# A two-layer hybrid backbone in float32r: work tiles at multiples of 2 KB in their partition

## The chip, the cores and the metric

One core of one Trainium2 chip. The time is device microseconds of one execution, the median of several runs. A core has TensorE (matmuls; PE in the views, its weight loads PEld), VectorE (DVE), ScalarE (ACT), GpSimd (POOL) and SyncE (SP, which issues loads here). Operands lie in SBUF, 128 partitions of which each holds a row of bytes. A tile has the same start address in every partition, and that address is what this case is about.

## The reference

A backbone for a generator over 256 latent tokens with 256 context tokens, width 1024, two layers. All weights and activations are float32. Of the code what is computed:

```python
for i in range(DEPTH):
    x = ffn_half_step(x, ...)            # s + 0.5 * m * (silu(h @ w1) * (h @ w3)) @ w2, d_ff 2816
    ctx = ffn_half_step(ctx, ...)
    h_c = modulate(rmsnorm(ctx, ...), ...)
    h = modulate(rmsnorm(x, ...), ...)
    p_l = split_columns(h @ w_in[i], IN_SIZES)     # and the same for h_c
    o_l, _, _ = gla_mixer(...)           # bidirectional chunked gated linear attention
    y = merge(h, (o_l, spatial_gating(...), fourier_mix(...), short_conv(...)), ...)
    x = x + m_lat[5] * y                 # merge: sum of sigmoid(h @ w_gate[k]) * (branch[k] @ w_branch[k]), @ w_out
    x = ffn_half_step(x, ...)
    # and the context stream likewise, but for the second layer's last steps
return rmsnorm(x, g_final)
```

## The kernel before

Activations stand with channels on partitions and tokens along the row: `x` is 128 x 8 x 512 (eight groups of 128 channels; the 256 latent and the 256 context tokens side by side). The second layer's later stages work on the latent half alone, so matmuls there have 256 columns instead of 512.

A float32 product is made of three float32r matmuls (line 317, in `passes`): each operand is split into a high part, rounded to float32r, and a low part, the rest; high by high, high by low and low by high are summed in PSUM. The streamed operand (`rhs`) is an activation: `hh`/`hl` is the normalised input of a stage, split; `gh`/`gl` the gated hidden units of a feed-forward block (and, from the same buffers, the branch outputs `b0h` to `b3l` and `mh`/`ml`); `mhi`/`mlo` the second half of the merged branches. The stationary operand (`lhsT`) is a 128 x 128 slice, 512 bytes of a row, of a weight tile. Only `natural` (line 863) has them the other way around: weights are streamed, `hh`/`hl` are stationary. Some small products stay in plain float32 (lines 643, 705, 744, 777, 778, 942, 984 to 995).

A weight tile is 128 x 1024 (4 KB of a row). SyncE loads it into one of four `raw` buffers, ScalarE rounds it into one of four `whi` (line 78), VectorE or GpSimd writes the rest into one of four `wlo` (line 81). The class `_Program` holds the order: units are listed in the order of the computation, each takes its weight tiles, and `ahead` and `release` issue loads and splits as ring places come free. Modulation vectors (`ada_unit`, line 286) are woven in between by a table of rates, and the attention scan (`gla_stream`) runs as a generator that is ticked by TensorE's issued columns.

SBUF tiles come from two pools, `const` and `work`. A pool lays its tiles one after the other in the order of their first use, `work` behind `const`. All tiles of one name and buffer number have one place. In the built program the starts are, in bytes within a partition:

| tiles (in this order) | start before | past a multiple of 2 KB | start after | past a multiple of 2 KB |
|---|---|---|---|---|
| `x` | 21952 | 1472 | 22528 | 0 |
| X, Y, F, Q, K, A of the scan; `ada_raw`, `mlo` in the same places | 38336 to 58816 | 1472 | 38912 to 59392 | 0 |
| `sq`/`aT`, `sq7`/`a2`, the five `tmp` buffers | 62912 to 75200 | 1472 | 63488 to 75776 | 0 |
| `hh`, `hl` | 77248, 93632 | 1472 | 77824, 94208 | 0 |
| two `ms` of 64 bytes | 110016, 110080 | 1472, 1536 | 21056, 21120 (in `const`) | 576, 640 |
| `raw`, `whi`, `wlo`, four of each | 110144 to 155200 | 1600 | 110592 to 155648 | 0 |
| `v`/`mhi`, the `gh`/`gl` buffers | 159296 to 196160 | 1600 | 159744 to 196608 | 0 |
| `Sa`, `wsgu`, `bsgu`, `z`/`m0` | 200256 to 208448 | 1600 | 200704 to 208896 | 0 |
| `bst`, `bag`, `lnr` | 216640 to 217152 | 1600, 1984, 64 | 217088 to 217600 | 0, 384, 512 |
| `four`/`m1`, `Sf` | 217216, 225408 | 128 | 217664, 225856 | 576 |

1472 and 1600 are both 64 past a multiple of 128. Slices within these tiles are at multiples of 512 or 1024 bytes from the start, in the largest weight tile of `natural` at multiples of 1152.

Of the kernel before, what the change touches and what calls it, by code (L numbers as in the profile page):

```python
# [7 lines left out]
F32 = mybir.dt.float32  # L8
# [10 lines left out]
CTX = (256, 256)  # L19
BOTH = (0, 512)  # L20
EPS = 1e-6
HOLD = 4
DPOOL = 1
HPOOL = ((), (0, 1, 2, 3), (0, 1))
# [151 lines left out]
def kernel(ctx: ExitStack, tc: tile.TileContext, I, out: bass.AP):  # L176
# [3 lines left out]
    cp = ctx.enter_context(tc.tile_pool(name="const", bufs=1))  # L180
    pool = ctx.enter_context(tc.tile_pool(name="work", bufs=1))
# [4 lines left out]
    def mm_ps(name="mm"):  # L186
        return ps.tile([128, 512], F32, tag="mm", name=name, bufs=5)

    def sm_ps(name="sm"):
        return ps.tile([128, 512], F32, tag="sm", name=name, bufs=3)  # L190
# [4 lines left out]
    def const(name, shape, eng=S):  # L195
        t = cp.tile(shape, F32, tag=name, name=name)
        eng.dma_start(out=t, in_=I[name])
        return t


    x = pool.tile([128, KT, 512], F32, tag="x", name="x")
    cvec = const("cvec", [128, KT, 2])
    ident = const("ident", [128, 128])
    gnorm = const("gnorm", [128, 6, KT])
    bada = const("bada", [128, 2, 72])
    ones = cp.tile([128, 128], F32, tag="ones", name="ones")
# [170 lines left out]
    class Norm:  # L377
# [6 lines left out]
        def ms(self, c):  # L384
            c0 = c[0]
            p = self.p[c] = sm_ps("ms")
            for u in range(2):
                for i, sq in enumerate((st8["sq"], st8["sq7"])):
                    T.matmul(p[:, u:u + 1], lhsT=sq[:, c0 + 128 * u:c0 + 128 * u + 128],
                             rhs=ones[:, 0:1], start=(i == 0), stop=(i == 1))  # L390
            ms = self.r = pool.tile([128, 16], F32, tag="ms", name="ms", bufs=2)
            V.tensor_scalar(ms[:, 0:2], p[:, 0:2], 1.0 / D, EPS, ALU.mult, ALU.add)
            G.tensor_tensor(ms[:, 2:4], ms[:, 0:2], mhalf[:, 0:2], ALU.pow)

# [136 lines left out]
    def add_ffn(l, s, m, streams, after, weave, nxt):  # L531
# [36 lines left out]
        def down(ds_, f0, nf, last):  # L568

            def fn(*ws):  # L570
                ps_ = [sm_ps("dn") if l == 0 and f0 == 0 and d > HOLD else mm_ps() for d in ds_]
                cuts = [(0, nf - 2), (nf - 2, 2)] if len(ds_) > 1 else [(0, nf)]
                for k0, n in cuts:
                    for w2, p in zip(ws, ps_):
                        passes(p, rng, w2, lambda k: gs[f0 + k0 + k], k0, n, k0 == 0, k0 + n == nf)
                        if k0 + n == nf:
                            P.release()
                for d, p in zip(ds_, ps_):
                    if l == 0 and f0 == 0 and d < HOLD:
                        gs["held"] = gs.get("held", []) + [(p, d)]  # L580
                        continue
                    for ph, dh in gs.pop("held", []):
                        residual(ph, dh, rng, gate)
                    residual(p, d, rng, gate)
                    if last:
                        add_sq(d, rng)
                        after(d, rng)
# [42 lines left out]
    def gla_stream(l, c, A, want_o):  # L630
# [142 lines left out]
        for u, Su in ((0, S0), (1, S1)):  # L773
            p = sm_ps("o")
            for h in range(4):
                hs = slice(128 * h, 128 * h + 128)
                T.matmul(p[:, hs], lhsT=M[:, u, h, :], rhs=v[:, 2 * st + u, hs], start=True, stop=False)
                T.matmul(p[:, hs], lhsT=Q[:, h, 128 * u:128 * u + 128], rhs=Su[:, h, :], start=False, stop=True)
            sq = Yf[:, 512 * u:512 * u + 512]
            S.activation(out=sq, in_=p, func=AF.Square)  # L780
            ms = pool.tile([128, 16], F32, tag="ms", name="oms", bufs=2)
            V.tensor_reduce(ms[:, 0:4], sq.rearrange("p (h e) -> p h e", h=4), mybir.AxisListType.X, ALU.add)
            V.tensor_scalar(ms[:, 4:8], ms[:, 0:4], 1.0 / 128, EPS, ALU.mult, ALU.add)
            G.tensor_tensor(ms[:, 8:12], ms[:, 4:8], mhalf[:, 0:4], ALU.pow)
            V.tensor_tensor(Wr[:, :, c0 + 128 * u:c0 + 128 * u + 128], p.rearrange("p (h e) -> p h e", h=4),
                            ms[:, 8:12].unsqueeze(2).to_broadcast([128, 4, 128]), ALU.mult)
            yield

    def gla_all(l, A, want_ctx):
        yield from gla_stream(l, CTX, A, want_ctx)  # L790
        yield
        yield from gla_stream(l, LAT, A, True)


    def add_mixer(l, both, after, weave, nxt):
# [120 lines left out]
        def spread():  # L916
            n = 4 * ntt
            A["rs"] = pool.tile([128, 16], F32, tag="lnr", name="lnr")
            V.tensor_scalar(A["rs"][:, 0:n], A["bag"][:, 0:n, 1], EPS, None, ALU.add)
            G.tensor_tensor(A["rs"][:, 0:n], A["rs"][:, 0:n], mhalf[:, 0:n], ALU.pow)  # L920
# [445 lines left out]
```

## Time and profile before

| | us |
|---|---|
| median of 3 runs | 2304.64 (2300.55 to 2306.05) |
| the profiled execution | 2305.67 |
| its span, first to last instruction | 2303.7 |
| TensorE busy | 2239.5 |
| VectorE, ScalarE, GpSimd busy | 1364.8, 770.8, 745.6 |
| granted TensorE clock, mean | 0.988 |

Busy time counts an engine's instructions from start to end; TensorE's overlap one another, since the next matmul begins while the one before drains, and their ends are modelled. The time a matmul costs is therefore the interval between two starts. In a view of stretches a count with (x384) divides a stretch of time into instructions. The order in which engines are listed says nothing on which one waits for which.

### The profile page before, as it was taken

The page shows a single profiled execution, that of the slowest core. Times are in us where ns is not written, and L with a number is a line of the kernel's source. Part 1 is how long each engine was busy: PE and PEld are TensorE (multiplying, and loading weights), DVE is VectorE, ACT ScalarE, POOL GpSimd, SP SyncE. Part 2 cuts the span into 40 slices and gives each one's busy share as a digit, 9 for nine tenths or more (in the row PEclk, how much of TensorE's full clock was granted, in tenths as well). Part 3 has the DMA queues.
Part 4 walks back from the last instruction along what each step waited for, and adds up shares of the span by engine and source line. Part 5 has one row for each costly group of instructions (what it writes and reads, how often), then busy time and mean ns, then how long its engine had stood idle before and what let it go on. Part 6 is the DMA issues. An engine that isn't in the chain of part 4 may idle for free. (4 is left out here: it accounts for less than half of the span.)

```text
span 2303.7 us, 31627 instructions
## 1 busy us (share of the span) xinstructions
PE 2239.5 (97%) x12718; PEld 1947.6 (85%) x12718; DVE 1364.8 (59%) x1857; ACT 770.8 (33%) x1090; POOL 745.6 (32%) x437
## 2 busy tenths in 40 slices
PE   6999999899999999999999999999999998999998
PEld 4888888898888888798888888888889998898998
DVE  3474575566656746863936555553536688875644
ACT  3322222443232223342222233222225553344443
POOL 1232324322203314142323253422335235524322
PEclk9999999999999999999999999999999999999999
DMA  7454454322222234523534433443635443475653
GB/s 268 156 168 143 130 178 139 125 83 67 87 85 83 83 106 149 201 98 126 178 121 155 148 108 128 136 148 112 207 110 172 136 156 117 140 262 196 228 186 117
DMA packets 98562, 330.43 MB, mean 143 GB/s; under 512 B 11504, under 2 KB 17648, under 8 KB 98160
## 3 DMA queue, kind: packets, MB, share of 16 engines
q1 hardware_dynamic: 90480, 315.91, 41.7%
q10 hardware_dynamic: 7936, 12.50, 1.5%
q8 instruction: 100, 1.64, 0.3%
q14 instruction: 46, 0.38, 0.1%
HBM read 322.08 MB, written 6.29 MB: 143 GB/s over the span
## 5 line engine op out<-in xcount | busy, mean ns | idle before, releaser
L317 PE MATMUL mm<-hh,whi 128*128 128x512 f32 (+1 forms) x2448 | 849.2, 351 | 3.4 <-ACT hh L425 2.3
L317 PE MATMUL mm<-hh,wlo 128*128 128x512 f32 (+1 forms) x2448 | 843.3, 349 | 6.5 <-DVE wlo L81 4.1
L317 PE MATMUL mm<-hl,whi 128*128 128x512 f32 (+1 forms) x2512 | 815.4, 346 | 0.2 <-POOL hl L435 0.2
L81 POOL TENSOR_TENSOR wlo<-raw,whi 128x1024 fp32r<-128x1024 f32 (+1 forms) x183 | 472.7, 2586 | 916.6 <-ACT whi L78 881.1
L78 ACT CAST whi<-raw 128x1024 fp32r<-128x1024 f32 (+2 forms) x458 | 469.3, 1032 | 766.2 <-PE mm L317 417.3
L81 DVE TENSOR_TENSOR wlo<-raw,whi 128x1024 fp32r<-128x1024 f32 (+3 forms) x275 | 349.3, 1275 | 363.3 <-ACT whi L78 360.0
L317 PEld LDWEIGHTS mm<-hh,wlo 128*128 128x128 f32 x2448 | 464.8, 190 | 71.8 <-DVE wlo L81 5.1
L317 PEld LDWEIGHTS mm<-hh,whi 128*128 128x128 f32 x2448 | 465.2, 190 | 67.4 <-ACT hh L425 3.3
L317 PEld LDWEIGHTS mm<-hl,whi 128*128 128x128 f32 x2512 | 451.8, 189 | 62.4 <-POOL hl L435 0.4
L286 DVE SCALAR_TENSOR_TENSOR ada_raw<-ada_raw,condb 128x1024 f32<-128x1024 f32 x128 | 253.9, 1986 | 15.3 <-DMA ada_raw<-in_wadaT_dram 12.0
L317 PE MATMUL mm<-gh,whi 128*128 128x512 f32 (+1 forms) x710 | 248.9, 351 | 0.0
L317 PE MATMUL mm<-gl,whi 128*128 128x512 f32 (+1 forms) x710 | 247.8, 349 | 0.0
L317 PE MATMUL mm<-gh,wlo 128*128 128x512 f32 (+1 forms) x710 | 247.7, 349 | 0.0
L543 DVE TENSOR_TENSOR g<-sg,mm 128x512 f32<-128x512 f32 (+1 forms) x88 | 54.6, 620 | 258.9 <-PE mm L317 254.5
L330 ACT CAST gh<-g 128x512 fp32r<-128x512 f32 (+1 forms) x88 | 50.0, 568 | 360.4 <-DVE g L543 360.4
L286 DVE SCALAR_TENSOR_TENSOR junk<-ada_raw,condb 128x1024 f32<-128x1024 f32 x96 | 145.2, 1513 | 11.1 <-DMA ada_raw<-in_wadaT_dram 11.0
L317 PEld LDWEIGHTS mm<-gl,whi 128*128 128x128 f32 x710 | 136.2, 192 | 17.1
L317 PEld LDWEIGHTS mm<-gh,whi 128*128 128x128 f32 x710 | 136.2, 192 | 17.0
L317 PEld LDWEIGHTS mm<-gh,wlo 128*128 128x128 f32 x710 | 136.1, 192 | 16.7
L527 DVE SCALAR_TENSOR_TENSOR x<-mm,mods,x 128x256 f32<-128x256 f32 x180 | 78.7, 477 | 30.6 <-PE mm L317 30.3
L331 DVE TENSOR_TENSOR gl<-g,gh 128x512 fp32r<-128x512 f32 (+1 forms) x88 | 58.9, 669 | 55.8 <-ACT gh L330 55.8
L362 POOL TENSOR_TENSOR sq<-sq,sqt 128x256 f32<-128x256 f32 (+1 forms) x44 | 51.3, 1165 | 104.0 <-ACT sqt L361 103.0
(222 smaller groups left out, 2360.3 us busy)
## 6 DMA issues: line engine op xcount, KB each, us to landing
raw<-in_w_dram SPq DMA_DIRECT2D x240, 512.0 KB, 3.6
ada_raw<-in_wadaT_dram SPq DMA_DIRECT2D x128, 512.0 KB, 4.4
raw<-in_wgate_dram SPq DMA_DIRECT2D x64, 512.0 KB, 3.6
raw<-in_winT_dram SPq DMA_DIRECT2D x56, 512.0 KB, 3.3
raw<-in_wbranch_dram SPq DMA_DIRECT2D x32, 512.0 KB, 3.7
raw<-in_w_dram SPq DMA_DIRECT2D x32, 384.0 KB, 3.2
ada_raw<-in_wada_dram SPq DMA_DIRECT2D x16, 512.0 KB, 6.5
raw<-in_wout_dram SPq DMA_DIRECT2D x16, 512.0 KB, 6.1
```

Source lines behind the costliest of these rows:

```text
L78: nc.scalar.copy(hi[:, :n], raw[:, :n])
L81: (eng or nc.vector).tensor_tensor(lo[:, :n], raw[:, :n], hi[:, :n].bitcast(F32), ALU.subtract)
L286: V.scalar_tensor_tensor(o, raw, 1.0, ada["c"][st], ALU.mult, ALU.mult, accum_out=mods[l][:, 8 * m + d, st:st + 1])
L317: T.matmul(acc[:, c0:c0 + cw], lhsT=a, rhs=b[:, c0:c0 + cw], start=bool(first and i == 0), stop=bool(last and i == n - 1))
L330: S.copy(dst_hi[:, a:b], src[:, a:b])
L331: V.tensor_tensor(dst_lo[:, a:b], src[:, a:b], dst_hi[:, a:b].bitcast(F32), ALU.subtract)
L362: eng.tensor_tensor(sq[:, a:b], sq[:, a:b], t[:, a:b], ALU.add)
L527: V.scalar_tensor_tensor(x[:, d, a:b], acc[:, a:b], gate(d, s[0] // 256), x[:, d, a:b], ALU.mult, ALU.add)
L543: V.tensor_tensor(g[:, a:b], sg[:, a:b], p3[:, a:b], ALU.mult)
```

## The change

A tile `pad` of 112 float32 (448 bytes) is allocated in `const` and never read or written. The tile `ms` (`ms` and `oms` by name, 16 float32, two buffers) is allocated from `const` instead of `work`. By these two the pool `work` begins 576 bytes later, and the tiles behind the former place of `ms` move by 448. No instruction is added, dropped or moved on any engine; each keeps its operands' tiles, shapes and waits. Addresses alone differ, as the table above shows. The tiles from `bag` on don't reach a multiple of 2 KB, and `four`/`m1` and `Sf`, which were at a multiple of 128, come to lie 64 past one. In `const`, `ident`, `ones` and `mhalf` come to a multiple of 128 and `cond` leaves one.

```diff
+PAD = 112
@@ in tile_hybrid_dit_kernel, behind const()
+    cp.tile([128, PAD], F32, tag="pad", name="pad")
@@ in Norm.ms
-            ms = self.r = pool.tile([128, 16], F32, tag="ms", name="ms", bufs=2)
+            ms = self.r = cp.tile([128, 16], F32, tag="ms", name="ms", bufs=2)
@@ in gla_stream
-            ms = pool.tile([128, 16], F32, tag="ms", name="oms", bufs=2)
+            ms = cp.tile([128, 16], F32, tag="ms", name="oms", bufs=2)
```

## Rows read from the trace of the kernel before

**Rows 1.** The page's busy time by engine: us, share of the span, instructions.

```profile
PE 2239.5 (97%) x12718; PEld 1947.6 (85%) x12718; DVE 1364.8 (59%) x1857; ACT 770.8 (33%) x1090; POOL 745.6 (32%) x437
```

**Rows 2.** Busy time by stretch: its length, each engine, granted clock, DMA share, GB/s.

```profile
100.00:600.00 500.00, 494.02 (x2546) 421.35 (x2545) 294.72 (x415) 149.30 (x209) 160.66 (x94) 0.99 0.39 125
600.00:1000.00 400.00, 397.34 (x1911) 329.62 (x1910) 258.51 (x324) 117.46 (x148) 110.62 (x72) 0.99 0.34 113
```

**Rows 3.** Line 317 alone in two stretches: length, PE busy (count), PEld busy (count), clock.

```profile
174.45:264.04 89.59, 89.59 (x385) 72.08 (x384) 1.00 0.37 123
264.04:307.57 43.53, 43.53 (x193) 36.04 (x192) 1.00 0.58 190
```

**Rows 4.** Groups by shape: out<-in, shapes, count | busy us, mean ns | idle before.

```profile
L317 PE MATMUL mm<-hh,whi 128*128 128x512 f32 x1408 | 558.3, 397 | 0.0
...
L317 PE MATMUL mm<-hh,whi 128*128 128x256 f32 x1040 | 290.8, 290 | 3.4 <-ACT hh L425 2.3 <-DVE y L1047 1.0
...
L317 PE MATMUL mm<-hl,whi 128*128 128x256 f32 x1104 | 259.6, 283 | 0.2 <-POOL hl L435 0.2
...
L317 PE MATMUL mm<-gh,whi 128*128 128x512 f32 x426 | 165.8, 389 | 0.0
L317 PE MATMUL mm<-gh,whi 128*128 128x256 f32 x284 | 83.1, 293 | 0.0
...
L863 PE MATMUL mm<-whi,hh 128*128 128x256 f32 x160 | 45.4, 284 | 0.0
...
L317 PE MATMUL dn<-gh,whi 128*128 128x512 f32 x48 | 18.7, 389 | 0.0
...
L446 PE MATMUL mm<-hh,wlo 128*128 128x256 f32 x64 | 12.8, 282 | 0.0
...
L995 PE MATMUL f<-four,f 128*128 128x256 f32 x48 | 11.7, 379 | 0.0
...
L643 PE MATMUL lg<-aT,a 32*128 32x256 f32 x32 | 8.0, 387 | 0.0
```

**Rows 5.** Timeline of TensorE, output projection of layer 0: start us, length us, instruction.

```profile
952.68 0.39 PE L317 MATMUL mm<-mhi,whi 128*128 128x512 f32 x1
952.90 0.40 PE L317 MATMUL mm<-mlo,whi 128*128 128x512 f32 x1
953.14 0.39 PE L317 MATMUL mm<-mhi,wlo 128*128 128x512 f32 x1
953.36 0.39 PE L317 MATMUL mm<-mhi,whi 128*128 128x512 f32 x1
953.59 0.40 PE L317 MATMUL mm<-mlo,whi 128*128 128x512 f32 x1
953.82 0.39 PE L317 MATMUL mm<-mhi,wlo 128*128 128x512 f32 x1
```

**Rows 6.** Timeline of TensorE, layer 1, 256 columns of `hh`; nine matmuls left out.

```profile
2201.79 0.28 PE L317 MATMUL mm<-hh,whi 128*128 128x256 f32 x1
...
2202.97 0.28 PE L317 MATMUL mm<-hl,whi 128*128 128x256 f32 x1
```

**Rows 7.** Timeline of TensorE, 256 columns of `gh`; six matmuls left out.

```profile
1364.36 0.28 PE L317 MATMUL mm<-gh,whi 128*128 128x256 f32 x1
...
1365.20 0.28 PE L317 MATMUL mm<-gl,whi 128*128 128x256 f32 x1
```

**Rows 8.** Timeline of TensorE, float32 matmuls, each recorded as two of half rate.

```profile
510.39 1.46 PE L995 MATMUL f<-four,f 128*128 128x256 f32 x6
...
473.91 1.99 PE L643 MATMUL lg<-aT,a 32*128 32x256 f32 x8
```

**Rows 9.** Line 330 on ScalarE: count, duration min/median/max ns, first and last start.

```profile
L330 ACT CAST mh<-m x8: 408/515/627, 899.0 to 2054.8; 128x512 fp32r<-128x512 f32 x4, 128x256 fp32r<-128x256 f32 x4
L330 ACT CAST mhi<-m x8: 407/514/622, 939.7 to 2074.7; 128x512 fp32r<-128x512 f32 x4, 128x256 fp32r<-128x256 f32 x4
```

**Rows 10.** Waits of the weight loads: engine line <- releaser: us in total, times, longest.

```profile
PEld ada L250 <- DMA ada_raw<-in_wada_dram: 14.6, 10, 3.2
```

## Prediction

> **What bounds the kernel now.** I read the share of busy time first, then the same by stretch, then the rate at which TensorE's matmuls follow each other, since the change moves no instruction and can act only through what one instruction takes. TensorE is busy for 2239.5 of 2303.7 us [rows 1], and in the long middle stretches it has hardly a gap: 494 of 500 and 397 of 400 us, while VectorE is busy for 59 and 65% there and ScalarE and GpSimd for less [rows 2]. So TensorE sets the time, and a nanosecond on its matmuls counts some eleven thousand times. Busy time of TensorE is modelled, however; what is to be read is the interval from one matmul to the next. Two neighbouring stretches give it. From 174.45 to 264.04 us every matmul streams `hh` or `hl` and 384 weight loads pass in 89.59 us: 233.3 ns for each matmul of 512 columns. From 264.04 to 307.57 us every one streams `gh` or `gl` and 192 pass in 43.53 us: 226.7 ns [rows 3]. The clock is 1.00 of 2.4 GHz in both, so 512 columns at one for each cycle would be 213.3 ns; the first sort spends 20 ns above that, the second 13.4.
>
> These two stretches do the same instructions in the same loop with weights from the same ring. What differs is where the streamed tile lies. By the address table above, `hh` and `hl` start at 1472 past a multiple of 2 KB, `gh` and `gl` at 1600, and the weight tiles `whi` and `wlo` at 1600 too. So `gh` is level with the weights (a multiple of 512 bytes apart) and `hh` is 128 bytes off. A second place tells this from "another stage": in the output projection, inside one accumulation and with the same weights, `mhi` (at 1600) and `mlo` (at 1472) take turns. The two matmuls that stream `mlo` and are followed by another row last 0.24 and 0.23 us until that one and are 0.40 long by the profile's model, those with `mhi` 0.22 to 0.23 and 0.39 [rows 5]. The difference follows the tile's place, not the stage. It is small in time and large in number.
>
> **The change part by part.** Nothing is added to an engine's queue, nothing leaves it, no wait moves: `pad` is never touched, and the two 64-byte `ms` tiles keep their two buffers in another pool, so what waits for them is as before. What is left are four sorts of address changes.
>
> (1) *Matmuls of 512 columns that stream `hh` or `hl`.* After the change streamed tile and weight tile both start at a multiple of 2 KB (each k-slice of the weights a multiple of 512 bytes further), so they are level, as `gh` and `whi` are today. There are three groups of 1408, one of them shown [rows 4], 4224 in all. If they take the interval of the level ones, each gains 233.3 - 226.7 = 6.6 ns [rows 3]: 27.9 us. The bounds: if the place has nothing to do with it, 0; if the level start at 0 brings them down to one column a cycle with little more, 233.3 - 216 = 17 ns each, 73 us (216 is the interval of the float32 matmuls, below). I take 27.9, because the nearest row, `gh` beside `whi`, already has the distance that all tiles will have.
>
> (2) *Matmuls of 256 columns that stream `hh` or `hl`, or hold them as weights.* Here the sign turns. Ten intervals with `hh` take 1.18 us, 118 ns [rows 6]; seven with `gh` take 0.84 us, 120 ns [rows 7]. Rounding leaves 1 to 2 ns; I take 1.0. There are 1040 + 1040 + 1104 of L317 (two of these groups shown), 2 x 64 of L446 and 3 x 160 of L863 [rows 4]: 3792, or +3.8 us. The bounds are -10 ns (one column a cycle and 2 ns more) and +2 ns.
>
> (3) *Float32 matmuls and the tiles that move the other way.* `four`, `m1` and `Sf` now lie at a multiple of 128 and come to lie 64 past one. The L995 matmuls stream `four`: six take 1.46 us, 0.38 of it the length of the last, so (1.46 - 0.38) / 5 = 216 ns each. The L643 ones stream `aT`, 64 past a multiple of 128 today: eight in 1.99 us, (1.99 - 0.39) / 7 = 229 ns with the first one's start-up in it [rows 4, 8]. They are some hundreds: 0 us, at most 48 x 13 ns = 0.6 us either way.
>
> (4) *VectorE, ScalarE, GpSimd and the DMAs.* The split of `m` on ScalarE reads `m0` (64 past) for `mh` and `m1` (at a multiple of 128) for `mhi`: medians 515 and 514 ns, longest 627 and 622 [rows 9]. One operand's place does nothing there; I take 0 for all three engines, and they have slack if it is a per cent [rows 2]. Of the loads TensorE notices those at the start, where its weight loads wait 14.6 us for `ada_raw` [rows 10]; a tenth of it either way would be 1.5 us. No row shows a load to another place; I take 0.
>
> The sum on TensorE: -27.9 + 3.8 = -24.1 us. The stretch of [rows 3] has DMA, VectorE and ScalarE well below full, so most reaches the end; in the mixer (600 to 1000 us, VectorE 258 of 400 [rows 2]) the scan's chain of VectorE and GpSimd work sets some of it, and I leave out a tenth: -21.7 us. The profiled execution takes 2305.67 us (its span of 2303.7 and 2.0 around it), 1.0 above the median of the three runs, so 2305.7 - 21.7 - 1.0 = **2283 us**.
>
> **A rule that speaks against it.** Rows 5 show two streamed tiles, both at multiples of 64 bytes, with different intervals beside the same weights. The Trainium skill, page "SBUF — State Buffer", section "Specifications (TRN2)", says that an access pays for crossing lines of 16 bytes; its section "Who interferes with whom" gives TensorE two independent read ports, for the streamed operand and for the weights. By that neither 1472, 1600 nor 0 differs for a contiguous float32 tile, terms 1 and 2 would be zero and the kernel would stay at 2304.6. The trace disagrees by 6.6 ns a matmul; the case is the second rival.
>
> **The rivals.** *All matmuls drop to one column a cycle.* Every fp32r matmul reads tiles that start 64 bytes past a multiple of 128, and the best interval exceeds 213.3 ns by 13.4. If that is the price of a first and a last piece cut by the start, and not of the weight load that runs beside each matmul, a start at 0 takes it away everywhere: 4224 x 17.3 + 1422 x 10.7 (`gh`, `gl`, with `dn`) + 3792 x 9.5 + 852 x 11 ns = 73 + 15 + 36 + 9 = 133 us, of which nine tenths give 2185 us. For it: 120 ns and 227 ns both lie 13 ns above 256 and 512 columns, whereas the float32 ones of L995, which take twice as long for a column, lie 3 ns above theirs [rows 8]. Against it: the unlevel 256-column ones lie *below* the level ones, which a cut start alone can't do; an overhead from two streams that meet fits both. The Trainium skill, page "TensorE: Matmul & The Clock Gate", section "Back-to-back issue gap", gives N / 2.4 + 2.5 ns for warm matmuls, 215.8 ns at 512; no run here shows that for fp32r, and by it the sum would be the one of this rival.
>
> *The place is not the reason*, but something that `hh` and `gh` differ in otherwise (who wrote them, which tile follows). Then nothing changes: 2304. Against it are the alternating `mhi` and `mlo` [rows 5].
>
> *Slower: 0 is the worse start.* What makes `gh` fast may be its own start (1600) and not its distance from the weights. If a start at 0, where streamed tile and weights begin on the same boundary, costs what 1472 costs today, `hh` gains nothing and `gh`, `gl` lose 6.6 ns: 1422 x 6.6 = 9.4 us on stages that TensorE bounds, about 2314 us; were `hh` to lose as much again, 2340. It decides when the intervals in the `gh` stretch rise above 230 ns. Rows can't exclude it: no fp32r tile starts at a multiple of 128 today.
>
> **How the numbers follow.** The forecast (2274 to 2297) gets 0.53; all matmuls at one column a cycle 0.15, something between the two 0.04; no difference 0.13; slower 0.15. A measurement of this kernel can tell about 0.3%, 7 us, from no change: faster 0.72, same 0.13, slower 0.15. The range leaves out the large gain and the worst of the slower case: 2258 to 2320.
>
> **What would show it.** In the profile of the changed kernel, 384 weight loads of the `hh` stretch in 87.1 us instead of 89.6, the `gh` stretch still 43.5, `mhi` and `mlo` alike, 256-column matmuls at 120 ns, and VectorE, ScalarE and GpSimd rows as before. The `gh` stretch is the judge: 41.5 us there means the large gain, over 44.2 the slower case. The prediction is wrong if `hh` and `gh` stay apart, or if the intervals become level and the end doesn't move, in which case the ring of weight tiles sets the pace.

## The result, and the profile after

The changed kernel takes 2276.61 us (median of 4 runs, 2275.03 to 2279.79), the kernel before beside it 2302.6 (4 runs, 2299.87 to 2306.05): a ratio of 0.9888, 95% interval 0.9868 to 0.9908, so 1.1% faster. The profiled execution takes 2279.79 us, its span is 2277.8, against 2305.67 and 2303.7 before. All lines inside the kernel function stand four further down: L317 is now L321, L330 is L334. Busy time by engine, which answers [rows 1]:

```profile
PE 2214.9 (97%) x12718; PEld 1950.2 (86%) x12718; DVE 1364.2 (60%) x1857; ACT 769.9 (34%) x1090; POOL 743.9 (33%) x437
```

The instructions are the same in number on each engine, and VectorE, ScalarE and GpSimd are busy as long as before. TensorE alone lost time, 24.6 us. The stretches of line 321 that answer [rows 3], and under them two of the last feed-forward block with 256 columns, first `hh`/`hl` and then `gh`/`gl` (length, PE busy and count, PEld busy and count, clock, DMA share, GB/s). Each stretch runs from the first matmul on one pair of tiles to the first on the other, 384 or 192 matmuls; the counts hold some that were still draining at the edge.

```profile
173.40:260.44 87.04, 87.04 (x385) 72.07 (x384) 1.00 0.39 127
260.44:303.96 43.52, 43.52 (x193) 36.04 (x192) 1.00 0.59 192
2145.95:2192.03 46.08, 46.08 (x386) 46.08 (x385) 1.00 0.59 184
2192.03:2215.07 23.04, 23.04 (x194) 23.04 (x193) 1.00 0.58 176
```

The same view of the kernel before for the stretches with 256 columns:

```profile
2172.23:2217.81 45.58, 45.58 (x387) 45.58 (x385) 1.00 0.57 186
2217.81:2240.84 23.03, 23.03 (x194) 23.03 (x193) 1.00 0.57 180
```

At 512 columns `hh` came down from 89.59 us to 87.04, from 233.3 ns a matmul to 226.7, and is now exactly at the pace of `gh`, which stayed at 43.52. At 256 columns `hh` went the other way, 45.58 to 46.08 us (118.7 to 120.0 ns), and `gh` stayed. In the output projection `mhi` and `mlo`, which took turns in [rows 5], are now alike (timeline of TensorE: start us, length us, instruction):

```profile
939.75 0.39 PE L321 MATMUL mm<-mhi,whi 128*128 128x512 f32 x1
939.98 0.39 PE L321 MATMUL mm<-mlo,whi 128*128 128x512 f32 x1
940.20 0.39 PE L321 MATMUL mm<-mhi,wlo 128*128 128x512 f32 x1
```

Where along the way the gain arises is read from a table by stages. Its bounds are the starts of the first matmul on each new `hh`: first feed-forward block, mixer of layer 0, second and third feed-forward block, mixer of layer 1, last block. Before (length, then PE, PEld, DVE, ACT, POOL busy, clock, DMA share, GB/s):

```profile
33.88:422.10 388.22, 380.53 (x1795) 317.37 (x1795) 218.29 (x285) 116.96 (x163) 132.01 (x62) 0.98 0.46 151
422.10:1006.46 584.36, 580.77 (x3073) 495.69 (x3073) 372.61 (x505) 187.78 (x258) 158.11 (x118) 0.99 0.32 106
1006.46:1384.20 377.74, 373.42 (x1756) 310.92 (x1756) 213.53 (x280) 107.42 (x148) 131.96 (x61) 0.99 0.42 137
1384.20:1755.00 370.80, 370.19 (x1757) 307.56 (x1756) 179.95 (x246) 107.13 (x148) 129.34 (x61) 1.00 0.44 145
1755.00:2100.17 345.17, 323.59 (x2610) 317.26 (x2610) 264.49 (x370) 158.87 (x237) 133.61 (x99) 0.98 0.51 166
2100.17:2303.70 203.53, 193.66 (x1594) 192.40 (x1594) 108.14 (x150) 86.32 (x128) 59.70 (x32) 0.97 0.54 176
```

After, the same stages:

```profile
33.08:416.05 382.97, 375.79 (x1794) 318.80 (x1795) 218.31 (x285) 116.85 (x163) 130.75 (x62) 0.98 0.47 153
416.05:992.87 576.82, 572.24 (x3074) 495.09 (x3073) 372.53 (x505) 187.59 (x258) 158.99 (x118) 1.00 0.33 107
992.87:1364.29 371.42, 367.13 (x1757) 310.64 (x1757) 213.43 (x280) 107.28 (x148) 131.54 (x61) 0.99 0.42 139
1364.29:1728.80 364.51, 363.90 (x1756) 307.68 (x1756) 179.01 (x246) 106.81 (x148) 128.35 (x61) 1.00 0.45 147
1728.80:2074.28 345.48, 324.40 (x2610) 318.39 (x2609) 264.73 (x370) 158.78 (x237) 133.51 (x99) 0.98 0.51 166
2074.28:2277.80 203.52, 193.75 (x1594) 192.97 (x1594) 108.41 (x150) 86.23 (x128) 59.90 (x32) 0.98 0.55 176
```

The four stages with 512 columns are 5.2, 7.5, 6.3 and 6.3 us shorter; the two with 256 columns alone, the mixer of layer 1 and the last block, are unchanged (+0.3 and 0.0). The start is 0.8 us shorter. Together that is 25.9 us, all of the difference in span. A feed-forward block holds 960 matmuls of 512 columns on `hh` and `hl`; at 6.6 ns they make 6.3 us, as the second and third block show.

Not all of the 25.9 us is the place of the tiles. TensorE's granted clock has two levels here, 2.4 GHz and half of it, and the profile has the lower one for 55.7 us of the span before and 46.7 after. In the first block it holds for 12.5 us before and 16.9 after, which takes from that block's gain; in the mixer of layer 0 for 6.83 and 3.41 us, which adds to that one's. The two stretches of the mixer, before and after (length, PE busy and count, clock, DMA share, GB/s):

```profile
961.16:967.99 6.83, 6.13 (x14) 0.50 0.71 277
951.12:954.53 3.41, 3.41 (x10) 0.50 0.56 210
```

The clock fell inside TensorE's wait of 2.7 us for `mhi` before, and 2.0 us behind the same wait after. Set against the mean interval of like matmuls at the full clock, the matmuls at half clock, pauses left out, cost 17.6 us before and 15.8 after. So about 1.8 of the 25.9 us is the clock, by this estimate; whether the change has a part in that is not shown.

### The profile page after: what moved, and what is told of

It reads as the page before. It is cut to its first block, busy times and chain, and to the rows that moved or that the text cites. A ratio compares the mean times of both kernels' runs of the same rounds, so it can differ in the third digit from the quotient of the medians.

```text
span 2277.8 us, 31627 instructions
## 1 busy us (share of the span) xinstructions
PE 2214.9 (97%) x12718; PEld 1950.2 (86%) x12718; DVE 1364.2 (60%) x1857; ACT 769.9 (34%) x1090; POOL 743.9 (33%) x437
## 4 chain that ended last, share of the span: by engine, by line
PE 84%; DVE 8%; issue 2%; DMA 2%; ACT 2%; POOL 2%; POOLq 0%; DVEq 0%; ACTq 0%; SPq 0%
PE mm L321 74%; PE mm L867 4%; PE dn L321 1%; DVE ada_raw L290 1%; PE lv L709 1%; DVE junk L290 1%; DVE wlo L82 1%; DMA ada_raw<-in_wadaT_dram 1%; ACT whi L79 1%; POOL wlo L82 1%; DMA x<-in_xT_dram 1%; ACT hh L429 1%; DMA raw<-in_w_dram 1%; PE mm L450 1%; PE ms L393 0%
## 5 line engine op out<-in xcount | busy, mean ns | idle before, releaser
L321 PE MATMUL mm<-hh,whi 128*128 128x512 f32 (+1 forms) x2448 | 843.8, 349 | 3.3 <-ACT hh L429 2.3
L321 PE MATMUL mm<-hh,wlo 128*128 128x512 f32 (+1 forms) x2448 | 837.8, 346 | 6.3 <-DVE wlo L82 4.1
L321 PE MATMUL mm<-hl,whi 128*128 128x512 f32 (+1 forms) x2512 | 808.9, 343 | 0.1
L321 PEld LDWEIGHTS mm<-hh,wlo 128*128 128x128 f32 x2448 | 468.5, 191 | 62.8 <-DVE wlo L82 5.1
L321 PEld LDWEIGHTS mm<-hh,whi 128*128 128x128 f32 x2448 | 469.0, 192 | 59.3 <-ACT hh L429 3.2
L321 PEld LDWEIGHTS mm<-hl,whi 128*128 128x128 f32 x2512 | 454.2, 190 | 54.3 <-POOL hl L439 0.3
L321 PE MATMUL mm<-gh,whi 128*128 128x512 f32 (+1 forms) x710 | 248.6, 350 | 0.0
L321 PE MATMUL mm<-gl,whi 128*128 128x512 f32 (+1 forms) x710 | 247.7, 349 | 0.0
L321 PE MATMUL mm<-gh,wlo 128*128 128x512 f32 (+1 forms) x710 | 247.5, 349 | 0.0
L334 ACT CAST gh<-g 128x512 fp32r<-128x512 f32 (+1 forms) x88 | 49.9, 567 | 352.0 <-DVE g L547 352.0
L321 PEld LDWEIGHTS mm<-gh,whi 128*128 128x128 f32 x710 | 136.1, 192 | 16.9
L321 PEld LDWEIGHTS mm<-gl,whi 128*128 128x128 f32 x710 | 136.0, 192 | 16.9
L321 PEld LDWEIGHTS mm<-gh,wlo 128*128 128x128 f32 x710 | 136.0, 191 | 16.5
L335 DVE TENSOR_TENSOR gl<-g,gh 128x512 fp32r<-128x512 f32 (+1 forms) x88 | 58.8, 668 | 55.7 <-ACT gh L334 55.7
```

The costliest lines, as they stand in the source:

```text
L321: T.matmul(acc[:, c0:c0 + cw], lhsT=a, rhs=b[:, c0:c0 + cw], start=bool(first and i == 0), stop=bool(last and i == n - 1))
L334: S.copy(dst_hi[:, a:b], src[:, a:b])
L335: V.tensor_tensor(dst_lo[:, a:b], src[:, a:b], dst_hi[:, a:b].bitcast(F32), ALU.subtract)
```

## The experiments

Three theories fit the result so far. *Distance*: a matmul's pace goes by how far its streamed tile starts from the weight tile, taken modulo 512 bytes; the change made all distances 0. *Own start*: 1472 past a multiple of 2 KB (448 past one of 512) is a bad start by itself. *Alignment*: what helps is that tiles begin at a multiple of 128 bytes or of 2 KB, as the change's words have it.

**Moving `ms` alone.** The change without its `pad`: all tiles are then level at 1600 past a multiple of 2 KB, 64 past a multiple of 128, and none is at a multiple of 2 KB.

```diff
-    cp.tile([128, PAD], F32, tag="pad", name="pad")
```

> Only the second part of the change: the two ms tiles move to the const pool, no pad. All tiles from x to lnr then start at 1600 past a multiple of 2 KB: level with the weights (distance a multiple of 512), but still 64 past a multiple of 128. Distance theory (the interval depends on the distance between streamed tile and weight tile): hh and hl at 226.7 ns, 256-column matmuls at 120 ns, about 2277 us. Own-start theory (a streamed tile at 1472, 448 past a multiple of 512, is slow by itself): 1600 is a good start, the same 2277 us. Alignment theory (a multiple of 128 or more is what helps): nothing of the gain, 2303 us, hh at 233.3 ns.

Measured: 2277.01 us (2275.29 to 2281.97), ratio 0.9899 (0.9883 to 0.9916). The `hh` stretch of this kernel, by the same view as above:

```profile
172.82:259.86 87.04, 87.04 (x386) 72.07 (x384) 1.00 0.39 127
```

The whole gain is there without one tile at a multiple of 2 KB or of 128 bytes. The alignment theory falls. What did it in the change was that two 64-byte tiles no longer lie between `hh` and the weights.

**All at the former bad start.** The changed kernel with a larger pad, so that everything is level at 960 past a multiple of 2 KB, which is 448 past a multiple of 512, the place modulo 512 that `hh` had before.

```diff
-PAD = 112
+PAD = 352
```

> The changed kernel with a larger pad, 352 float32: all tiles from x to lnr start at 960 past a multiple of 2 KB. That is 448 past a multiple of 512, as 1472 is, and 64 past a multiple of 128; streamed tiles and weights are level. Distance theory: 226.7 ns for hh and gh, 2277 us. Own-start theory: hh stays at 233.3 ns, and gh, gl and the branch tiles go to 233.3 ns too, 2312 us. Alignment theory: no gain, 2303 us or more.

Measured: 2277.73 us in one run. The `hh` stretch:

```profile
176.53:263.57 87.04, 87.04 (x385) 72.07 (x384) 1.00 0.39 127
```

The start of `hh` is as before modulo 512, and its pace is that of the changed kernel: the own-start theory falls.

**Only `hh` and `hl` level.** The kernel before, with 128 bytes ahead of `hh` and 384 behind `hl`; `x`, the scan's tiles and `tmp` stay at 1472.

```diff
+            pool.tile([128, 32], F32, tag="padh0", name="padh0")
             st8["hh"] = pool.tile([128, KT, 512], F32R, tag="hh", name="hh", bufs=1)
             st8["hl"] = pool.tile([128, KT, 512], F32R, tag="hl", name="hl", bufs=1)
+            pool.tile([128, 96], F32, tag="padh1", name="padh1")
```

> The kernel before with 128 bytes ahead of hh and 384 behind hl, unused: hh and hl go to 1600, weights and gh to 64 past a multiple of 2 KB (a multiple of 512 further), everything ahead of hh stays at 1472, ms stays in work. So hh and hl alone become level. Distance and own-start theory: the whole gain, 2277 us, with only mlo still 128 bytes off. Alignment theory: 2303 us. If part of the gain came from x, the tmp buffers or the scan's tiles at their new places: between the two, 2280 to 2295.

Measured: 2280.11 us (2277.85 to 2283.34), ratio 0.991 (0.9894 to 0.9926). The `hh` stretch:

```profile
173.53:260.57 87.04, 87.04 (x385) 72.07 (x384) 1.00 0.39 128
```

The place of two tiles carries the gain, 22.5 us of the 26.0 by the medians, and by the spans of the profiled executions 27.7 against 25.9. Here too the clock has a part: it was at half for 39.8 us, which cost 13.3 us by the estimate above, against 17.6 in the kernel before. Without that the two gains are 23.4 and 24.1 us; the spread is too wide to say whether the other tiles contribute.

**`hh` off by 128 in an otherwise changed kernel.** All tiles at multiples of 128 bytes as the change puts them, but 384 bytes ahead of `hh` and 128 behind `hl`; weights at 0 modulo 512, `hh` at 384.

```diff
+            pool.tile([128, 96], F32, tag="padh0", name="padh0")
             st8["hh"] = pool.tile([128, KT, 512], F32R, tag="hh", name="hh", bufs=1)
             st8["hl"] = pool.tile([128, KT, 512], F32R, tag="hl", name="hl", bufs=1)
+            pool.tile([128, 32], F32, tag="padh1", name="padh1")
```

> The changed kernel with 384 bytes ahead of hh and 128 behind hl, unused: all tiles at multiples of 512 as in the changed kernel, hh and hl 128 bytes below a multiple of 512, at a multiple of 128. Distance theory: the distance of before is back, hh and hl at 233.3 ns, their 256-column matmuls at 118.7, 2303 us. Own-start theory: 384 is neither the bad 448 nor 64; if multiples of 128 are good, 2277 us. Alignment theory (multiples of 128): 2277 us; (only multiples of 512 or 2 KB): 2303 us.

Measured: 2303.04 us (2297.41 to 2305.92, 10 runs), ratio 0.9999 (0.9986 to 1.0012). The stretches of `hh` and `gh` with 512 columns, and of `hh` with 256:

```profile
174.74:264.33 89.59, 89.59 (x385) 72.07 (x384) 1.00 0.37 124
264.33:307.87 43.54, 43.54 (x194) 36.03 (x192) 1.00 0.60 192
2169.92:2215.49 45.57, 45.57 (x386) 45.57 (x385) 1.00 0.57 186
```

The gain is gone, and each stretch is that of the kernel before to the hundredth (89.59 in [rows 3]; 45.58). Neither the start of `hh` nor its alignment brings that about, since the two runs with all tiles 64 past a multiple of 128 had the worse alignment and the better time. The distance does.

Distance from what? `x`, the scan's tiles and `tmp` are level with `hh` in the kernel before, where `hh` is slow, and off it in the run that moves `hh` and `hl` alone, where it is fast, so it isn't them. `raw` always lies as the weights do, and other engines and DMAs use it while TensorE runs. But they aren't needed for the price: in the `hh` stretch of the kernel before, 25 intervals have no instruction of VectorE, ScalarE or GpSimd and no DMA packet under way, with a mean of 233.6 ns, and the other 359 have 233.3 (in the changed kernel 226.8 and 226.7). What is left of the tiles that were at one place with `raw` are TensorE's own weights.

**Other distances.** The next five kernels, one run each, move `hh`/`hl` and the `gh`/`gl` buffers in the changed kernel by pads of the same sort, so that each gives two distances (streamed tile less weight tile, modulo 512). Four rows stand for each: `hh` and `gh` with 512 columns (384 and 192 matmuls), then with 256 (384 and 192).

> The changed kernel with hh and hl moved to 256 past a multiple of 512 bytes and the gh/gl buffers to 64 past one; the weight tiles stay level at 0. It measures two more distances of the streamed tile from the weights (0 and 384 are known: 226.7 and 233.3 ns at 512 columns). 'Near in either direction hurts' (the cost grows as the two streams come closer to meeting, largest around 256): the 384 loads of the hh stretch take more than 89.6 us, the gh stretch of 192 about 44 us. 'Level or not' (one price for whatever isn't level): hh stretch 89.6 us, gh stretch 44.8 us (233.3 ns each), the whole about 2312 us. 'Only 384 is bad' (a property of one distance): hh 87.1, gh 43.5, the whole 2277 us.

`hh` at 256, `gh` at 64: 2282.26 us, beside 2305.51 for the kernel before.

```profile
172.74:259.83 87.09, 87.09 (x385) 72.07 (x384) 1.00 0.39 127
259.83:303.80 43.97, 43.97 (x194) 36.06 (x193) 1.00 0.58 192
2148.53:2194.60 46.07, 46.07 (x386) 46.07 (x385) 1.00 0.57 186
2194.60:2217.22 22.62, 22.62 (x195) 22.62 (x193) 1.00 0.58 179
```

None of the three expectations holds for both tiles: the first is right on `gh` alone, the third on `hh` alone. 256 is as good as level, so neither nearness nor "level or not" is the rule, and 64 has a price of its own (229.0 ns) between the two known ones.

> hh and hl at 128 past a multiple of 512 bytes (the mirror of the kernel before, whose hh are 128 short of one), gh/gl at 32. Symmetric theory: hh stretch 89.6 us as before, about 2303 to 2312 us in all. One-sided theory (it matters which stream runs ahead): hh 87.1 us or less, 2277 us or a little less. gh at 32: level-or-not says 44.8 us for 192, a theory in which small distances are free 43.5 us.

`hh` at 128, `gh` at 32: 2310.72 us beside 2305.51.

```profile
177.97:267.57 89.60, 89.60 (x386) 72.08 (x385) 1.00 0.36 123
267.57:312.37 44.80, 44.80 (x194) 35.98 (x193) 1.00 0.57 188
2178.89:2224.45 45.56, 45.56 (x386) 45.56 (x385) 1.00 0.58 188
2224.45:2246.86 22.41, 22.41 (x195) 22.41 (x193) 1.00 0.59 182
```

128 is 384 over again at both widths, as the symmetric theory has it, and 32 bytes off level already cost the full 6.6 ns.

> hh and hl at 64 past a multiple of 512 bytes, gh/gl at 192. Level-or-not: hh 89.6 us, gh 44.8 us, 2312 us. A price that depends on the distance modulo 128 rather than 512: hh as bad as or worse than before, gh the same as hh for each matmul. Free small distances: hh 87.1, and the run shows whether gh at 192 resembles 128 or 256.

`hh` at 64, `gh` at 192: 2290.99 us beside 2305.51.

```profile
176.37:264.26 87.89, 87.89 (x385) 72.12 (x384) 1.00 0.38 124
264.26:309.05 44.79, 44.79 (x193) 36.09 (x192) 1.00 0.59 190
2160.77:2206.00 45.23, 45.23 (x387) 45.23 (x385) 1.00 0.59 189
2206.00:2227.77 21.77, 21.77 (x195) 21.77 (x194) 1.00 0.61 186
```

64 costs 228.9 ns and 192 costs 233.3 at 512 columns: the distance modulo 128 isn't the rule. The last row is the fastest of all with 256 columns: 113.4 ns.

> hh and hl at 448 (64 short of a multiple of 512 bytes), gh/gl at 320. Symmetric theory: hh as at 64, gh as at 192 in the run beside this one. One-sided theory: they differ. Level-or-not: 89.6 us for 384 of hh, 44.8 for 192 of gh, 2312 us. Should some distance lie below the level 226.7 ns, the 13 ns above one column a cycle are in part a matter of place too; if none does, they are not.

`hh` at 448, `gh` at 320: 2302.18 us beside 2305.51.

```profile
175.69:265.28 89.59, 89.59 (x385) 72.19 (x384) 1.00 0.37 124
265.28:309.23 43.95, 43.95 (x193) 36.06 (x192) 1.00 0.57 190
2169.96:2215.18 45.22, 45.22 (x386) 45.22 (x385) 1.00 0.57 187
2215.18:2237.80 22.62, 22.62 (x195) 22.62 (x193) 1.00 0.59 183
```

The symmetric theory falls: 448 is not like 64, and 320 not like 192. But 448 is like 192, and 320 like 64.

> The changed kernel with hh and hl 96 past a multiple of 512 bytes in all stages and the gh/gl buffers 160 past one. At 256 columns 96 took 120.0 ns, as level does, while 32 took 116.7. If 96 is like level in general, hh keeps 226.7 ns at 512 columns, 384 loads of its stretch in 87.1 us and the whole about 2277 us (gh apart): then 'level with the weights' is one of several good distances, and a rule in plain steps of 128 or 512 bytes doesn't hold. If the price at 512 columns goes by the distance modulo 128 or 64 (32 and 96 alike), 233.3 ns, 89.6 us, and about 2305 us. gh at 160 (also 32 past a multiple of 128): by the first 192 loads in 43.5 us, by the second 44.8.

`hh` at 96, `gh` at 160: 2312.07 us beside 2309.92.

```profile
176.03:265.65 89.62, 89.62 (x386) 72.08 (x384) 1.00 0.38 122
265.65:310.63 44.98, 44.98 (x194) 36.16 (x192) 1.00 0.59 193
2178.44:2224.52 46.08, 46.08 (x387) 46.08 (x386) 1.00 0.57 186
2224.52:2247.04 22.52, 22.52 (x194) 22.52 (x193) 1.00 0.61 177
```

At 512 columns `hh` has the 233.3 ns of the second theory and `gh` 234.3, a little above it; the first falls, though 96 looks level at 256 columns (120.0 ns). The two widths have to be measured each for itself. Put together, as the stretch by the number of matmuls:

| distance modulo 512 | 512 columns, ns | 256 columns, ns |
|---|---|---|
| 0, 256 | 226.7, 226.8 | 120.0, 120.0 |
| 32 | 233.3 | 116.7 |
| 64, 320 | 228.9 to 229.0 | 117.8, 117.8 |
| 96 | 233.4 | 120.0 |
| 128, 384 | 233.3, 233.3 | 118.6, 118.7 |
| 160 | 234.3 | 117.3 |
| 192, 448 | 233.3, 233.3 | 113.4, 117.8 (both paces occur at both, below) |

Each of the four pairs that are 256 bytes apart has one pace at 512 columns, so the distance theory holds with 256 in place of 512. Level is the best place that was found for 512 columns and one of the worst for 256.

**Level for 512 columns, off level for 256.** Since layer 1 has matmuls of 256 columns alone from its mixer on, their operands can lie further along the row in the same tiles. The changed kernel, with `hh`/`hl` as views into rows that are 512 bytes longer, and `gh`, `b0` to `b3` and `m` in columns 48 to 303 instead of 0 to 255 there; 192 bytes in the first kernel, 448 in the second, 96 in the third (its core):

```diff
+HS, GS = 48, 48
-    def new_h():
-        st8["hh"] = pool.tile([128, KT, 512], F32R, tag="hh", name="hh", bufs=1)
-        st8["hl"] = pool.tile([128, KT, 512], F32R, tag="hl", name="hl", bufs=1)
+    def new_h(s=0):
+        for n in ("hh", "hl"):
+            t = pool.tile([128, KT * 512 + 128], F32R, tag=n, name=n, bufs=1)
+            st8[n] = t[:, s:s + KT * 512].rearrange("p (k t) -> p k t", t=512)
...
-        return h[:, i % 2, :], l[:, i % 2, :]
+        return h[:, i % 2, s:], l[:, i % 2, s:]
```

> The changed kernel, with the operands of the stages that have 256 columns alone (layer 1 from its mixer on: hh, hl, b0 to b3, m, mhi/mlo, the last block's gh/gl) placed 192 bytes further within their tiles; everything of 512 columns stays level. 3648 matmuls of 256 columns get distance 192, and nothing else moves. Distance theory with two paces: at 192 a 256-column matmul takes 113.4 or 117.8 ns instead of 120, so 3648 x 2.2 to 6.6 = 8 to 24 us less, about 2261 us (2253 to 2269) against 2277 of the changed kernel; the 384 loads of the last block's hh stretch 43.5 to 45.2 us instead of 46.1. Rival, level is best everywhere: 2277 or more. Rival, the mixer of layer 1 is not bound by TensorE: only the last block's 1584 matmuls count, 3.5 to 10 us, 2267 to 2274.

Measured: 2271.76 us (2265.57 to 2275.44, 5 runs), ratio 0.9856 (0.9836 to 0.9876). The `hh` and `gh` stretches of the last block, by the view of its matmul line:

```profile
2142.20:2187.43 45.23, 45.23 (x386) 45.23 (x385) 1.00 0.57 188
2187.43:2210.05 22.62, 22.62 (x195) 22.62 (x194) 1.00 0.55 183
```

And its last two stages, the mixer of layer 1 and the last block:

```profile
1726.50:2070.59 344.09, 318.65 (x2611) 312.17 (x2610) 264.81 (x371) 158.89 (x238) 132.70 (x99) 0.97 0.51 167
2070.59:2272.30 201.71, 191.02 (x1594) 189.03 (x1594) 108.99 (x150) 86.33 (x128) 59.91 (x32) 0.97 0.54 178
```

> As the run beside it with 448 bytes (64 short of a multiple of 512) instead of 192. If the pace depends on the distance modulo 128 alone (64, 192, 320, 448 alike), the same two paces and about the same time, 2261 us (2253 to 2269). If the distance also decides which of the two paces a run of matmuls settles in, the share of 113.4 ns runs differs from that at 192, and the time with it by up to some 10 us.

Measured: 2272.86 us (2267.45 to 2276.35), ratio 0.9868 (0.985 to 0.9885): no different from 192. Both paces occur here too.

> As the two beside it with 96 bytes, a distance that wasn't tried. If it is like 32 (116.7 ns at 256 columns, odd multiple of 32): 3648 x 3.3 = 12 us less than the changed kernel, about 2265 us, with an interval that cycles through several values. If like 64: two paces, 2253 to 2269. If like 128: 118.7 ns, about 2272 us.

Measured: 2278.81 us in one run; 120.0 ns, as level, which none of its three cases had:

```profile
2145.06:2191.14 46.08, 46.08 (x386) 46.08 (x385) 1.00 0.57 184
```

The forecast of 2261 us was missed by 11. The pace did change: over the trace the 2544 matmuls on `hh` and `hl` that moved to 192 have a mean of 115.7 ns where they follow each other without a stop, about half of them at 113.4 and half at 117.8. But of some 14 us less for TensorE (3648 times about 4 ns) 3.2 reach the end. In the mixer of layer 1, TensorE's intervals, pauses and the cost of half clock left out, came down by 9.0 us, and the stage is 1.4 us shorter (345.48 to 344.09). TensorE was busy for 324 of 345 us there, so part of the pace is lost in waits: its pauses grew by 4.4 us. The largest part is the wait for `K` from VectorE (TensorE's waits in this stage, changed kernel and this one):

```profile
PE kt L739 <- DVE K L718: 4.9, 2, 3.5
PE kt L741 <- DVE K L720: 6.7, 2, 3.7
```

So the rival on that mixer was right, but waits are not all of it. The granted clock was at half for 19.1 us of this stage (19.2 in the kernel with 448) and for 10.4 in the changed kernel, the 0.97 and 0.98 of the rows; against like matmuls at the full clock that costs 3.2 us more. One of these stretches begins at 1839.85 us, behind a wait for `K` that grew to 2.98 us. In the last block the matmuls happened on the slow of the two paces: its `gh` at 192 takes 22.62 us here and 21.77 in the kernel with `hh` at 64 above, with the same distance, shapes and weights. There 4.1 us came off the intervals, pauses and half clock took 1.0 each, and the block gains 1.8 us (203.52 to 201.71). What decides which of the two paces a run of matmuls falls into stays open. Against the changed kernel, the medians say 4.9 us less, measured at different times beside their own runs of the kernel before; the intervals of the two ratios overlap (0.9868 to 0.9908, and 0.9836 to 0.9876), so that it beats the changed kernel is likely and not shown.

## Why the prediction was right

The forecast was 2283 us, range 2258 to 2320; measured were 2276.61, faster by more than the 0.3% that can be told. Its mechanism was the right one.

*Term 1*, 4224 matmuls at 6.6 ns: right in size where it was read (2.55 us for 384 is 6.6 ns each), a little high as a whole. Added up over the trace, the intervals of these matmuls came down from 986.7 us to 960.7, by 26.0 instead of 27.9. Not every stretch ran at 233.3 before: two of 288 took 66.9 us, 232.4 ns each, which is 0.5 us of the difference. The other 1.4 are in the mixer, whose 1344 matmuls came down from 234.6 to 229.1 ns, by 5.6 and not 6.6.

*Term 2*, +1.0 ns for 3792 matmuls of 256 columns: the sign was right, against what one would expect of a better place. Measured were +1.3 ns in the stretch above, and +2.7 us for the 3184 on `hh` and `hl` as streamed tiles (409.4 to 412.1 us, what they ran at half clock included).

*Term 3*: the float32 matmuls kept their time. Those on `four`, which now starts 64 past a multiple of 128, have (1.89 - 0.38) / 7 = 216 ns, as in [rows 8]; the timeline of TensorE:

```profile
504.48 1.89 PE L999 MATMUL f<-four,f 128*128 128x256 f32 x8
```

*Term 4*: the split on ScalarE that read one operand at a multiple of 128 and one 64 past it has the medians of [rows 9], 514 and 512 ns:

```profile
L334 ACT CAST mh<-m x8: 406/514/623, 886.4 to 2028.3; 128x512 fp32r<-128x512 f32 x4, 128x256 fp32r<-128x256 f32 x4
L334 ACT CAST mhi<-m x8: 405/512/622, 926.8 to 2048.2; 128x512 fp32r<-128x512 f32 x4, 128x256 fp32r<-128x256 f32 x4
```

At the start TensorE's weight loads waited 12.9 us for `ada_raw` instead of 14.6 in [rows 10], and the first `hh` matmul began 0.8 us earlier, within the 1.5 that the bound had left for that.

*The tenth left out* was too much, but not for nothing. TensorE's sum was forecast at -24.1 us. Added up over the trace from start to start, pauses and half clock included, the intervals changed by -26.0 and +2.7 us on `hh` and `hl` as streamed tiles, by -0.9 on `gh` and `gl`, by -0.6 on the branch and `m` tiles (which no term held), and by +0.6 in `natural` and L450: -24.2 in all. That this meets the forecast so closely is in part luck: the first two terms came out smaller than forecast, and 1.5 us come from tiles that had no term. I took 2.4 us as lost behind VectorE and GpSimd in the mixer. The span became 25.9 us shorter, so 21.7 was 4.2 us too little. That isn't the tenth alone: 0.8 is the start, and about 1.8 is the clock, which no term held. Without both some 23.3 us are left, 1.6 more than 21.7 and 0.8 less than the sum of 24.1. Something was lost, and in the mixer: of 8.9 us for 1344 matmuls at 6.6 ns the mixer of layer 0 shows 7.5, though the clock gave it 1.5. By the view of waits TensorE has one of 0.8 us for `wlo` there that the kernel before has not; the run with `hh` and `hl` alone level has it too, and the one with `hh` off by 128 has none. The 4.2 are two thirds of the 6.4 us between forecast and result; the other 2.2 are how the profiled execution lies to the median, 3.2 us above it after and 1.0 before.

*The rivals.* All matmuls at one column a cycle: the `gh` stretch, named as the judge, would have taken 41.5 us and took 43.52. Tiles that start at 0 pay the same 13.4 ns over 213.3 as those that start 64 past a multiple of 128, so a first and last piece cut by the start is not what they pay for. Slower, because 0 is the worse start: the stretch would have been over 44.2. The place is not the reason: refuted twice, by the result and by the run that is off by 128, 26 us apart with the same instructions.

The prediction weighed two rules of the Trainium skill. By "SBUF — State Buffer", sections "Specifications (TRN2)" and "Who interferes with whom", with independent ports for the streamed operand and the weights, no place here should have mattered; the runs disagree, since 128 bytes between the two make 226.7 or 233.3 ns. By "TensorE: Matmul & The Clock Gate", section "Back-to-back issue gap", 512 columns take 215.8 ns; no stretch of 192 or more fp32r matmuls of that width came under 226.7 at a granted clock of 1.00.

One thing in the prediction was right by luck in its form: "level" was put as a multiple of 512 bytes apart. The period is 256, by the four pairs tried, which no row of before could tell, since only the distances 0 and 384 occurred.

## What to carry to other kernels

Where a kernel's time is a row of like matmuls, read the interval from start to start, by operand and by width, and compare stretches that do the same work on different tiles: a few nanoseconds between them times some thousands are worth a look at the address table. What counted here was the distance between the streamed tile and the weight tile modulo 256 bytes, not the alignment of either; a small tile allocated between the two is enough to spoil it, and moving that tile away was the whole fix. Level was best at 512 columns and not at 256, so measure each width, and ask where TensorE is the bound before counting the gain.

## What the runs showed that was not expected

The price has a period of 256 bytes in the four pairs tried at 512 columns, and is neither symmetric nor a matter of nearness: at 512 columns 64 costs 2.2 ns over level, 192 costs 6.6, 256 nothing.

Off level the intervals are not steady. In the `hh` stretch of the kernel before nearly all lie at 229 to 230 or at 237 to 238 ns; in that of the changed kernel all lie between 225 and 228. With 256 columns and an odd multiple of 64 there are two steady paces, 113.4 and 117.8 ns, and one stretch holds one of them for hundreds of matmuls: 21.77 and 22.62 us for 192 at the same distance.

The 13 ns above one column a cycle that level matmuls pay at both widths are not a fixed part of a matmul: at 256 columns the better pace off level has 113.4 - 106.7 = 6.7 ns. At 512 columns no distance tried had less than 13.4. Tried were the multiples of 32 up to 192, and 256, 320, 384 and 448; 224 and the odd multiples of 32 above it were not. Why the distance matters is not shown by any of this: that the stream of a matmul and the weight load beside it hinder each other fits, and no run separates the two.
